# Block inverses of a delta rule by one VectorE transpose instead of through DRAM, with longer allowances for small transfers

## The chip, the core and the metric

The kernel runs on one core of a Trainium2 chip. The core has a TensorE (PE; its weight loads are shown apart as PEld), a VectorE (DVE), a ScalarE (ACT), a GpSimd (POOL) and a SyncE (SP), which here only issues DMAs. The engines run on their own and wait for each other through semaphores. The metric is the device time of one execution in microseconds (us); lower is better.

## The reference

One decoder layer on 512 positions of width 1024, in float32: `h = x + 1/2 FFN1(norm(x))`, `h = h + mixer(norm(h))`, `h = h + 1/2 FFN2(norm(h))`, and a last norm. Each FFN is a SwiGLU with an inner width of 2816. The mixer projects `h` to many columns, runs two recurrences over the positions, projects each one's output back, merges the two with sigmoid gates and projects once more. One recurrence is HGRN2 with 8 heads. The other, the gated delta rule, has 16 value heads over 8 query/key heads of width 128 and is cut to:

```python
# q, k, v in chunks of C = 64 positions; gam = cumsum(g), L = exp(gam_t - gam_s) for s <= t
A = strict_lower((k * beta) @ k.T * L)
T = inverse(eye + A)                       # unit lower triangular, one per head and chunk
u = T @ (v * beta)
w = T @ (k * beta * exp(gam))
qk = q @ k.T * L
for each chunk:                            # S: 128 x 128, carried along
    v_new = u - w @ S
    o = (q * exp(gam)) @ S + qk @ v_new
    S = S * exp(g_end) + k_to_end.T @ v_new
```

The change is about `T`. The mathematics are the same before and after.

## The kernel before, in words

Every large product is made of three float32r products: each operand is split into a high and a low part (`uh`, `ul`; `whi`, `wlo`), and `mm3` (lines 164 to 166) issues high x high, low x high and high x low, a "triple". Weights come from HBM in slabs of 128x512 (`raw`); ScalarE casts the high part (L1394 in the mixer, L159 outside of it) and VectorE subtracts it for the low part (L1396, L160). Three `raw` buffers and five pairs of split slabs are in flight.

The mixer is one long list of work, made on the host while the program is built. Each activity is a Python generator that yields what it needs next: `"get"` a buffer, `"on"` an event, `"use"` an engine for an estimated time, or `"lag"`, a time that passes without an engine, which stands for a DMA in flight. The class `Desk` plays these generators against a clock of its own and issues each instruction when its engine is free by that clock. So the estimates decide only the order in which each engine's instructions stand. On the chip each engine runs its own list strictly in that order and waits where something is not there yet. `LAG` holds the times for transfers. `SLACK = 0.8` lets TensorE's steps other than the large products stand 0.8 us later than the clock says they are ready. The thread `product` fills TensorE with projections wherever no other step is ready; `loader` and `maker` bring its slabs.

The delta rule works on eight units `u` of two value heads, in four blocks of 128 positions. Of a unit these activities touch the change:

- `g_e` loads the decay sums broadcast to all partitions (`gb`, L796) and makes `exp(-|gb - gam|)` of them on ScalarE (L801, L804).
- `g_n` makes the negated strict lower matrix `n2` on VectorE (L874).
- `g_b` inverts the 32x32 diagonal blocks. Four DMAs store the diagonal blocks to DRAM (`nb`, L893), four load them back spread over partitions (`m`, shown as `gfs`, L899), and one loads a piece of the identity (`t`, shown as `ft`, L904). GpSimd then runs 31 steps of substitution of two instructions each (L910, L911). After it a DMA of GpSimd stores `t` to DRAM (`nt`, L914), and four of SP load it with rows and columns exchanged (`tq`, shown as `gln`, L923).
- `g_inv` waits for that. VectorE copies it into `tp` (L947) and transposes each of four 32-row groups into `ut` (L954); ScalarE copies pieces (L960). Two levels of small products on TensorE (L971, L981, L994, L1002), with copies between them on ScalarE (L974, L984, L996, L1005), join the inverted blocks, first two of 32 rows and then two of 64.
- `g_rec` is the recurrence over the four blocks, with `pw`, `pog`, `pks` for its accumulators (L1056 to L1085), VectorE's scaling (L1074), and at its end the output norm and two transposes `pto` on TensorE (L1129) that go to DRAM by `keep` (L1151).

Other activities with small transfers are `tgate` (L1162, L1165: gates `tg`, stored by `keep`), `branch` (`yh`, stored by `keep`), `operand` (loads a stored head output `og`, L1200, and splits it, L1206 and L1208) and `merged` (loads `mi`, `mt`, `mg`, L1227 to L1233, and merges, L1236 to L1242). `claim` hands buffers of the HGRN2 heads to the delta rule once those are done.

Of the kernel before, what the change touches and what calls it, by code (L numbers as in the profile page):

```python
# [8 lines left out]
F32 = mybir.dt.float32  # L9
# [7 lines left out]
P = 128  # L17
T = 512
NT = T // P
D = 1024  # L20
# [20 lines left out]
WB = 5  # L41
TA = 6
RB = 3
KEEP = 2
CONVS = 5
SLACK = 0.8
LAG = dict(raw=3.2, gb=4, nb=5, m=6, nt=4, tq=8, out=4)
EASE = 2.5
LANES = {"a": 2, "b": 2, "d": 1, "e": 1}

# [319 lines left out]
def mixer(tc, mp, e):  # L370
# [67 lines left out]
    od = dr.tile([VH, P, T], F32, name="od")  # L438


    D = Desk(mm=2, a=2, b=2, d=1, e=1, ta=TA, tm=6, thg=1, raw=RB, w=WB, tq=1, n2=2, gz=2, fs=1, ut=1, kn=3, gm=1,
             qm=2, gb=2, ln=1, mi=3, mt=3, at=4, vb=4, t64=2, on=2, ft=1, x=1, we=1, w_=1, s=3)
    V = lambda n: ("use", "DVE", 0.21 + 0.001 * n)
    A = lambda n: ("use", "ACT", 0.2 + 0.0009 * n)
# [439 lines left out]
    def g_b(u, st):  # L884


        n2 = st["n2"]
        nb = dr.tile([4, 8, 32, 32], F32, name=f"nb{u}")
        nt = dr.tile([4, 32, 32, 8], F32, name=f"nt{u}")
        for b in range(4):  # L890
            r = slice(32 * b, 32 * b + 32)
            yield S
            sp.dma_start(nb[b].rearrange("s i j -> i s j"), n2[r, :, :, r].rearrange("p a c j -> p (a c) j"))  # L893
        yield "lag", LAG["nb"]
        yield "on", *([("P", u - 1)] if u else ["m"])
        m = G["m"][0]
        for b in range(4):
            yield S
            sp.dma_start(m[32 * b:32 * b + 32].rearrange("p i j -> p (i j)"),  # L899
                         nb[b].rearrange("s i j -> s (i j)").unsqueeze(0).to_broadcast([4, 8, 1024]))  # L900
        yield "get", "ft", 1
        t = places["ft"]("ft", (P, 32, 8))
        yield S
        sp.dma_start(t, eye4)  # L904
        yield "lag", LAG["m"]
        for j in range(31):
            n, w = 31 - j, j // 4 + 1
            yield "use", "POOL", .7 + .004 * n * w
            tv = v3(places["fm"]("fm", (P, 96))[:, :n * w], n)
            pool.tensor_tensor(tv, bc(m[:, j + 1:, j], w), t[:, j:j + 1, :w].to_broadcast([P, n, w]), op=ALU.mult)  # L910
            pool.tensor_tensor(t[:, j + 1:, :w], t[:, j + 1:, :w], tv, op=ALU.add)  # L911
        D.fire(("P", u))
        yield "use", "POOL", .6
        pool.dma_start(nt.rearrange("b q i c -> (b q) i c"), t)  # L914
        yield "lag", LAG["nt"]
        D.put("ft")
        D.fire(("T", u))
        yield "on", "tq"
        yield "get", "tq", 1
        tq = st["tq"] = G["tq"][0]  # L920
        for b in range(4):
            yield S
            sp.dma_start(tq[32 * b:32 * b + 32], nt[b].rearrange("q i c -> i q c"))  # L923
        yield "lag", LAG["tq"]
        D.fire(("B", u))

    def g_w(u, i, st):
        yield "on", ("v", 2 * u + i), ("C", u)
# [10 lines left out]

    def g_inv(u, st):  # L940

        yield "on", ("B", u), *([("I", u - 1)] if u else []), *([("K", u - 3)] if u > 2 else []), \
            ("ut", u % 3), ("t64", u % 2), *(["more"] if u else [])
        n2 = st["n2"].rearrange("p a c b -> p (a c) b")
        tp = G["tp"][u % 2]
        yield V(256)
        dve.tensor_copy(tp.rearrange("p s (c g) -> p s c g", g=4), st["tq"].rearrange("p (g s) c -> p s c g", g=4))  # L947
# [243 lines left out]
    def operand(k, wait, get, make):  # L1191

        yield "on", *wait
        if get:
            yield "get", get, 2
        yield "on", ("od", k), *([("so", k - 2)] if k > 10 else [])
        yield "get", "ta", 1
        yield S
        og = ta("og")
        sp.dma_start(og, od[k])  # L1200
        yield "lag", LAG["raw"]
        if k > 8:
            yield "on", "projected"
        yield *A(512), 1
        a, b = so[k] = make()
        act.copy(a, og)  # L1206
# [14 lines left out]
    def merged(d):  # L1221
# [64 lines left out]
    def claim(name, tag, n, shape, zero=False):  # L1286

        G.setdefault(name, [])
        yield "on", ("free", tag)
        for j in range(n):  # L1290
            yield "get", "w_" if tag == "w" else tag, 1
            G[name].append(pl(tag, shape))
            if zero:
                yield "use", "POOL", 1.0
                pool.memset(G[name][-1], 0.0)
            if tag == "ln":
                D.fire("tq")
            elif tag == "fs":
                D.fire("m")
            else:  # L1300
                D.fire((name, j))
# [197 lines left out]
        D.start((2, i), h_pair(i))  # L1499
    for name, tag, n, shape in (("kn", "kn", 3, tb), ("qm", "qm", 2, tb), ("n2", "n2", 2, big),  # L1500
                                ("gz", "gz", 2, (P, NT, 256)), ("at", "at", 4, tb), ("vb", "vb", 4, tb),
                                ("m", "fs", 1, (P, 32, 32)), ("tq", "ln", 1, (P, 32, 8)), ("x", "x", 1, col),
                                ("we", "we", 1, col), ("w", "w", 1, col)):
        D.start((6, 0), claim(name, tag, n, shape))
    D.start((6, 0), claim("ut", "ut", 1, (P, 8, P), True))
# [106 lines left out]
```

## Time and profile before

| | |
|---|---|
| median of 3 runs | 1676.11 us (1674.88 to 1676.27) |
| profiled execution | 1671.58 us |
| its span, first to last instruction | 1669.8 us |
| mean granted TensorE clock | 0.994 |
| busy share of the span | PE 98%, PEld 83%, DVE 58%, ACT 42%, POOL 19% |
| DMA | 181.21 MB in 141223 packets, 53008 of them under 512 B |

The mixer's slabs are loaded from 357.1 us on (L1377); its last output, by the product with `wo` (L1536), is added to `h` at 1292.3 us. In the profile a line "engine line out<-in" names an instruction by its output and input tiles; `SPq` and `POOLq` are the queues in which DMAs are issued. An entry in brackets, `[4.56 <-DVE gut L954]`, gives the idle time of the engine just before the instruction and what ended it. A row of waits has the total, the number and the longest. Busy shares are averages over stages with different limits, and on an engine which is not the limit idle time costs nothing.

### The profile page before, as it was taken

Reading aid. Unit: us, or ns where it says so; the run is one execution under the profiler, and the core shown is the slowest. Engines: PE = TensorE matmul, PEld = TensorE weight load, DVE = VectorE, ACT = ScalarE, POOL = GpSimd, SP = SyncE. Lnnn points to the kernel's source line nnn. Section 1 sums busy time; section 2 is a strip of 40 time slices with the busy share of each in tenths; the row PEclk is TensorE's granted clock in tenths of the full one; section 3 lists DMA queues with packets and bytes.
Section 4 is the critical chain, followed back from the end, with each engine's and each line's share of the span. In section 5 each row is a group of like instructions: output and inputs, shape, how many; then the busy total and the mean of one; then the engine's idle time right before and its main releaser. Section 6 shows DMA issues by size and latency. Waiting matters only on the chain. (4 is left out here: it accounts for less than half of the span.)

```text
span 1669.8 us, 27534 instructions
## 1 busy us (share of the span) xinstructions
PE 1640.4 (98%) x10130; PEld 1392.4 (83%) x10130; DVE 969.9 (58%) x2000; ACT 699.3 (42%) x1547; POOL 322.1 (19%) x637
## 2 busy tenths in 40 slices
PE   8999999999999999989999999999999999999997
PEld 6888888888888898868988888887888888888886
DVE  5544443337677777648878888755445444444333
ACT  5333332333334346446665565554224333333332
POOL 2000000001121221461655346600001000000001
PEclk9999999999999999999999999999999999999998
DMA  5232233332212222543344343445544232223333
GB/s 175 90 100 95 96 97 108 117 119 71 77 65 63 79 83 77 154 132 80 112 111 117 112 121 109 137 141 183 160 150 133 90 100 95 98 98 92 98 98 108
DMA packets 141223, 181.21 MB, mean 109 GB/s; under 512 B 53008, under 2 KB 58640, under 8 KB 141088
## 3 DMA queue, kind: packets, MB, share of 16 engines
q1 hardware_dynamic: 140272, 177.78, 34.4%
q8 instruction: 80, 1.31, 0.3%
q0 software_dynamic: 384, 1.05, 0.2%
q10 hardware_dynamic: 432, 0.62, 0.1%
q14 instruction: 55, 0.45, 0.1%
HBM read 163.11 MB, written 16.29 MB: 107 GB/s over the span
## 5 line engine op out<-in xcount | busy, mean ns | idle before, releaser
L164 PE MATMUL pmm<-uh,whi 128*128 128x512 f32 (+1 forms) x1280 | 516.4, 404 | 10.2 <-ACT whi L301 6.9
L166 PE MATMUL pmm<-uh,wlo 128*128 128x512 f32 (+1 forms) x1280 | 501.5, 392 | 0.0
L165 PE MATMUL pmm<-ul,whi 128*128 128x512 f32 (+1 forms) x1280 | 501.2, 392 | 0.0
L159 ACT CAST whi<-raw 128x512 fp32r<-128x512 f32 (+1 forms) x290 | 176.5, 609 | 404.9 <-PE pmm L165 382.9
L160 DVE TENSOR_TENSOR wlo<-raw,whi 128x512 fp32r<-128x512 f32 (+1 forms) x290 | 203.1, 702 | 243.3 <-ACT whi L159 242.6
L164 PEld LDWEIGHTS pmm<-uh,whi 128*128 128x128 f32 (+1 forms) x1280 | 241.4, 189 | 59.7 <-ACT whi L301 7.4
L166 PEld LDWEIGHTS pmm<-uh,wlo 128*128 128x128 f32 (+1 forms) x1280 | 241.0, 188 | 52.5 <-DVE wlo L302 0.5
L165 PEld LDWEIGHTS pmm<-ul,whi 128*128 128x128 f32 (+1 forms) x1280 | 241.6, 189 | 46.4
L1396 DVE TENSOR_TENSOR wlo<-raw,whi 128x512 fp32r<-128x512 f32 x241 | 168.5, 700 | 150.4 <-ACT whi L1394 143.2
L1394 ACT CAST whi<-raw 128x512 fp32r<-128x512 f32 x241 | 149.3, 620 | 244.5 <-PE pmm L165 160.1
L202 POOL TENSOR_TENSOR acc<-acc,sqt 128x512 f32<-128x512 f32 x24 | 32.4, 1352 | 805.6 <-ACT sqt L200 805.3
L164 PE MATMUL pnat<-whi,uh 128*128 128x256 f32 x512 | 155.2, 303 | 0.0
L166 PE MATMUL pnat<-whi,ul 128*128 128x256 f32 x512 | 144.7, 283 | 0.0
L165 PE MATMUL pnat<-wlo,uh 128*128 128x256 f32 x512 | 144.5, 282 | 0.0
L164 PE MATMUL pmm<-gh,whi 128*128 128x512 f32 (+1 forms) x374 | 141.0, 377 | 0.0
L166 PE MATMUL pmm<-gh,wlo 128*128 128x512 f32 (+1 forms) x374 | 140.9, 377 | 0.0
L165 PE MATMUL pmm<-gl,whi 128*128 128x512 f32 (+1 forms) x374 | 140.8, 377 | 0.0
L910 POOL TENSOR_TENSOR fm<-gfs,ft 128x60 f32<-128x60 f32 (+24 forms) x248 | 95.9, 387 | 127.7 <-DMA ft<-hmask 89.0
L911 POOL TENSOR_TENSOR ft<-ft,fm 128x60 f32<-128x60 f32 (+24 forms) x248 | 99.3, 400 | 19.4
L164 PEld LDWEIGHTS pnat<-whi,uh 128*128 128x128 f32 x512 | 97.6, 191 | 2.1
L165 PEld LDWEIGHTS pnat<-wlo,uh 128*128 128x128 f32 x512 | 97.8, 191 | 0.8
L166 PEld LDWEIGHTS pnat<-whi,ul 128*128 128x128 f32 x512 | 97.5, 190 | 0.0
(384 smaller groups left out, 2180.4 us busy)
## 6 DMA issues: line engine op xcount, KB each, us to landing
raw<-wt SPq DMA_DIRECT2D x128, 256.0 KB
raw<-w1b SPq DMA_DIRECT2D x88, 256.0 KB
raw<-w1a SPq DMA_DIRECT2D x86, 256.0 KB
raw<-wn SPq DMA_DIRECT2D x64, 256.0 KB
raw<-w2b SPq DMA_DIRECT2D x45, 256.0 KB
raw<-w2a SPq DMA_DIRECT2D x40, 256.0 KB
raw<-wbg SPq DMA_DIRECT2D x32, 256.0 KB
gb<-gtd SPq DMA_DIRECT2D x16, 256.0 KB
```

The source lines that it names most:

```text
L159: act.copy(hi[:, :f], raw[:, :f])
L160: dve.tensor_tensor(lo[:, :f], raw[:, :f], hi[:, :f].bitcast(F32), op=ALU.subtract)
L164: pe.matmul(pt, ah, bh, start=first, stop=False)
L165: pe.matmul(pt, ah, bl, start=False, stop=False)
L166: pe.matmul(pt, al, bh, start=False, stop=last)
L202: pool.tensor_tensor(acc, acc, s, op=ALU.add)
L910: pool.tensor_tensor(tv, bc(m[:, j + 1:, j], w), t[:, j:j + 1, :w].to_broadcast([P, n, w]), op=ALU.mult)
L911: pool.tensor_tensor(t[:, j + 1:, :w], t[:, j + 1:, :w], tv, op=ALU.add)
L1394: act.copy(hi, raw)
L1396: dve.tensor_tensor(lo, raw, hi.bitcast(F32), op=ALU.subtract)
```

## The change

After GpSimd's last step, `t` holds in each group of 32 partitions four column groups `g` by eight matrices `s`, and on the free axis 32 rows by eight columns. Now one VectorE transpose, which works in blocks of 32x32, reads `t` with its free axes exchanged and writes the rows to partitions and `(c, g, s)` straight into `tp`. The store `nt`, the loads `tq` and the copy are gone. `t` has three buffers now (`t0` in the place of `ft`, two in `t12` in the place where `tq` was) and is given back after the transpose. `g_inv` waits for the event `P`, which is fired behind GpSimd's last step, instead of `B`.

The allowances change too: `raw` from 3.2 to 3.5, `gb` from 4 to 6.5, `nb` from 5 to 6, `m` from 6 to 7, `out` from 4 to 5; `nt` and `tq` go; and the loads of `operand` and `merged`, which were given `raw`, are given a time of their own, `back`, of 6.

```diff
-LAG = dict(raw=3.2, gb=4, nb=5, m=6, nt=4, tq=8, out=4)
+LAG = dict(raw=3.5, gb=6.5, nb=6, m=7, out=5, back=6)
...
-    D = Desk(mm=2, a=2, b=2, d=1, e=1, ta=TA, tm=6, thg=1, raw=RB, w=WB, tq=1, n2=2, gz=2, fs=1, ut=1, kn=3, gm=1,
+    D = Desk(mm=2, a=2, b=2, d=1, e=1, ta=TA, tm=6, thg=1, raw=RB, w=WB, n2=2, gz=2, fs=1, ut=1, t=3, kn=3, gm=1,
...
         nb = dr.tile([4, 8, 32, 32], F32, name=f"nb{u}")
-        nt = dr.tile([4, 32, 32, 8], F32, name=f"nt{u}")
...
-        yield "get", "ft", 1
-        t = places["ft"]("ft", (P, 32, 8))
+        yield "on", ("t12", 0) if u % 3 else ("t0", 0)
+        yield "get", "t", 1
+        t = st["t"] = G["t12"][0][:, u % 3 - 1] if u % 3 else G["t0"][0]
         yield S
         sp.dma_start(t, eye4)
         yield "lag", LAG["m"]
...
         D.fire(("P", u))
-        yield "use", "POOL", .6
-        pool.dma_start(nt.rearrange("b q i c -> (b q) i c"), t)
-        yield "lag", LAG["nt"]
-        D.put("ft")
-        D.fire(("T", u))
-        yield "on", "tq"
-        yield "get", "tq", 1
-        tq = st["tq"] = G["tq"][0]
-        for b in range(4):
-            yield S
-            sp.dma_start(tq[32 * b:32 * b + 32], nt[b].rearrange("q i c -> i q c"))
-        yield "lag", LAG["tq"]
-        D.fire(("B", u))
...
-        yield "on", ("B", u), *([("I", u - 1)] if u else []), *([("K", u - 3)] if u > 2 else []), \
+        yield "on", ("P", u), *([("I", u - 1)] if u else []), *([("K", u - 3)] if u > 2 else []), \
...
         yield V(256)
-        dve.tensor_copy(tp.rearrange("p s (c g) -> p s c g", g=4), st["tq"].rearrange("p (g s) c -> p s c g", g=4))
-        D.put("tq")
+        dve.transpose(tp.rearrange("p s (c g) -> p c g s", g=4), st["t"].rearrange("p i c -> p c i"))
+        D.put("t")
...
         sp.dma_start(og, od[k])
-        yield "lag", LAG["raw"]
+        yield "lag", LAG["back"]
...
         sp.dma_start(g, td[8 + d])
-        yield "lag", LAG["raw"]
+        yield "lag", LAG["back"]
```

In the list of buffers that `claim` hands over, `("tq", "ln", 1, (P, 32, 8))` becomes `("t0", "ft", 1, (P, 32, 8))` and `("t12", "ln", 1, (P, 2, 32, 8))`.

More of the change, by code (lines that the diff above doesn't have):

```diff
@@ L1295, in claim @@
                 pool.memset(G[name][-1], 0.0)
-            if tag == "ln":
-                D.fire("tq")
-            elif tag == "fs":
+            if tag == "fs":
                 D.fire("m")
@@ L1501, in mixer @@
                                 ("gz", "gz", 2, (P, NT, 256)), ("at", "at", 4, tb), ("vb", "vb", 4, tb),
-                                ("m", "fs", 1, (P, 32, 32)), ("tq", "ln", 1, (P, 32, 8)), ("x", "x", 1, col),
+                                ("m", "fs", 1, (P, 32, 32)), ("t0", "ft", 1, (P, 32, 8)), ("t12", "ln", 1, (P, 2, 32, 8)), ("x", "x", 1, col),
                                 ("we", "we", 1, col), ("w", "w", 1, col)):
```

## The prediction

> **What bounds the kernel now.** I read the page first, then the waits of TensorE, then the stretches in which it waited, then the four engines in time around the longest wait.
>
> ```profile
> span 1669.8 us, 27534 instructions
> PE 1640.4 (98%) x10130; PEld 1392.4 (83%) x10130; DVE 969.9 (58%) x2000; ACT 699.3 (42%) x1547; POOL 322.1 (19%) x637
> ```
>
> The page says TensorE is busy in 98% of the span. Busy is no proof of work without gaps, so the waits come next (engine and line, what it waited for, us in total, times, longest).
>
> ```profile
> PE pmm L164 <- ACT whi L301: 6.9, 1, 6.9
> PE pq L971 <- DVE gut L954: 5.2, 2, 4.6
> PE pmm L164 <- DVE tg L1162: 2.4, 1, 2.4
> PE pog L1083 <- DVE x L1074: 1.7, 1, 1.7
> PE pq L981 <- ACT acc L974: 1.5, 1, 1.5
> ```
>
> The wait on L301 lies in the first stage, which the diff doesn't touch. The other four lie in the mixer, and they are all that TensorE waits for there, so the change can gain only these four, what the clock adds to them, and whatever it does to the order of the products. Here are the four stretches (stretch; PE busy, PEld, DVE, ACT, POOL; granted clock, DMA share, GB/s).
>
> ```profile
> 700.00:750.00 50.00, 44.77 (x259) 35.94 (x258) 23.66 (x41) 21.59 (x49) 35.10 (x88) 0.93 0.44 130
> 850.00:900.00 50.00, 48.50 (x404) 44.35 (x404) 40.95 (x96) 32.07 (x95) 29.09 (x70) 1.00 0.34 92
> 1000.00:1050.00 50.00, 48.29 (x393) 43.36 (x392) 42.77 (x98) 26.59 (x78) 28.96 (x70) 1.00 0.38 107
> 1150.00:1200.00 50.00, 47.64 (x207) 38.99 (x206) 28.19 (x48) 18.04 (x31) 0.00 (x0) 0.97 0.53 168
> ```
>
> TensorE lacks 5.2, 1.5, 1.7 and 2.4 us of the 50, and in the first and the last stretch the clock fell too, to 0.93 and 0.97 on average. Why the longest one came about is seen engine by engine: SP's queue, then ScalarE, then VectorE, then TensorE (start, us, instruction, idle before it and releaser).
>
> ```profile
> 721.18 5.87 SPq L923 DMA_DIRECT2D gln<-nt  x4
> 728.18 0.42 SPq L796 DMA_DIRECT2D gb<-gtd  x1
> ```
> ```profile
> 733.09 1.28 ACT L801 ACTIVATE x<-gb,gx 128x128 f32<-128x128 f32 x4 [5.59 <-DMA gb<-gtd]
> ```
> ```profile
> 735.57 0.69 DVE L1396 TENSOR_TENSOR wlo<-raw,whi 128x512 fp32r<-128x512 f32 x1 [5.61 <-ACT whi L1394]
> 736.29 1.36 DVE L954 STREAM_TRANSPOSE gut<-gtp 32x256 f32<-32x256 f32 x3
> ```
> ```profile
> 736.78 0.24 PE L971 MATMUL pq<-gut,gn 32*32 32x32 f32 x2 [4.56 <-DVE gut L954]
> 737.70 1.05 PE L971 MATMUL pq<-gut,gn 32*32 32x32 f32 x30 [0.68 <-DVE gut L954]
> 739.28 0.63 PE L165 MATMUL pmm<-ul,whi 128*128 128x512 f32 x1
> 739.71 0.63 PE L166 MATMUL pmm<-uh,wlo 128*128 128x512 f32 x1
> 743.55 0.63 PE L166 MATMUL pmm<-uh,wlo 128*128 128x512 f32 x1
> 745.06 0.39 PE L165 MATMUL pmm<-ul,whi 128*128 128x512 f32 x1
> 745.29 0.40 PE L166 MATMUL pmm<-uh,wlo 128*128 128x512 f32 x1
> ```
>
> Four small loads `gln<-nt`, which bring the first block inverse back from DRAM, hold SP's queue for 5.87 us. The load `gb<-gtd` behind them is issued at 728.18. ScalarE comes to its consumer L801 and stands 5.59 us. The slabs' casts are behind it, VectorE stands 5.61 us for a cast, three of the four transposes of the same block inverse are behind that, and TensorE, at the first product of the inverse, stands 4.56 and then 0.68 us. After that the products are slow: from 739.28 to 743.55 lie ten intervals between starts, 0.43 us each, and from 745.06 to 745.29 it is 0.23 us.
>
> The other three waits have the same root, a small transfer that landed after its consumer's turn in the list:
>
> ```profile
> ACT gat L801 <- DMA gb<-gtd: 5.5, 2, 3.3
> 1036.67 0.62 ACT L1206 CAST sogm<-og 128x512 fp32r<-128x512 f32 x1 [2.71 <-DMA og<-od]
> 1039.32 0.35 DVE L1074 TENSOR_SCALAR x<-pw,gx 128x128 f32<-128x128 f32 x1 [0.44 <-ACT x L1026]
> DVE tg L1162 <- DMA td<-tg: 5.6, 1, 5.6
> ```
>
> ScalarE waited twice more for `gb`, up to 3.3 us, and L974, for which the products at L981 waited 1.5 us, is in its queue behind one of these. The 2.7 us for `og` end at 1036.67, L1074 follows on VectorE at 1039.32, and TensorE's 1.7 us at L1083 are put down to L1074; that `og` is their root I infer from the times. The 5.6 us that VectorE stood for the store `td<-tg` precede the 2.4 us at L164 directly: the step that reads the accumulator out was waiting for room. The list allows 4 us for `gb`, 3.2 for `og` and 4 for the store.
>
> **The change, part by part.** Its first part takes the way through DRAM out.
>
> ```profile
> L947 DVE COPY gtp<-gln x4: 381/386/395, 729.1 to 1045.8; 128x256 f32<-128x256 f32 x4
> L947 DVE COPY x<-gln x4: 371/384/391, 773.6 to 1090.0; 128x256 f32<-128x256 f32 x4
> L954 DVE STREAM_TRANSPOSE gut<-gtp x8: 432/435/442, 729.5 to 1047.6; 32x256 f32<-32x256 f32 x8
> L914 POOL DMA_DIRECT2D nt<-ft x8: 625/626/759, 716.0 to 1079.5; - x8
> L923 SPq DMA_DIRECT2D gln<-nt x32: 319/562/3493, 721.2 to 1084.4; - x32
> ```
>
> Removed are 8 stores (L914), 0.626 us of GpSimd each, 5.0 us in all; 32 loads on SP (L923), 0.56 us each in the median and up to 3.49; and 8 copies of 0.385 us on VectorE. Added are 8 transposes of 128x256. Their nearest row is the transpose of 32x256 at 0.435 us with as many elements per partition, so VectorE gains 8 x 0.05 = 0.4 us of work; it is 47% to 86% busy in the stretches above, and the estimate's ends are 0.385 us (the copy's price) and four times 0.435 us (if the four groups of 32 partitions went one after the other), which would be +10.8 us on VectorE, 1.35 us a unit, mostly in slack. I take 0.435 as the instruction handles all partitions like the copy does.
>
> The latency it removes is longer: from the issue of the store to the copy were 13.1 us in the first unit (716.0 to 729.1) and 10.5 in the last (1079.5 to 1090.0). That is no gain by itself, as TensorE had other products to do. But the four loads block no `gb` any more, and this wait goes too:
>
> ```profile
> SPq L923 <- DMA nt<-ft: 10.6, 3, 4.2
> ```
>
> SP stood 10.6 us for the stores, with slab loads behind it; those had cover in five slab buffers, so I cost this at nothing.
>
> The second part is the new times. `gb` gets 6.5 us instead of 4, `og` and the merge's three loads 6 instead of 3.2, stores 5 instead of 4, slabs 3.5 instead of 3.2, and the loads before GpSimd's loop 6 + 7 instead of 5 + 6. None of these makes an engine wait by itself; they move the consumers later in the list and let other products go ahead. TensorE's order still has 7,533 rows against 7,535, so the work is the same; 8 DMA issues leave GpSimd's order.
>
> What each wait is worth: the first is 4.56 + 0.68 us, and the ten slow intervals, 4.27 us instead of 2.3, so 2.0, with some 0.7 (an estimate) for the products at both edges of the slow stretch: 7.9. The second 1.5, the third 1.7. The fourth is 2.4 and the clock: 0.97 over 50 us is 3 us at half speed, so 1.5 us of work lost: 3.9. Sum 15.0 us. For the fourth the new allowance looks short: VectorE's wait for the store alone is 5.6 us, and stores are given 5. [...]
>
> What is new: the first transpose of a unit now waits for GpSimd's last step directly, where 10.5 to 13.1 us lay between. It is issued in VectorE's strict order, with the slabs' subtractions behind it, for which TensorE waits.
>
> ```profile
> L910 POOL TENSOR_TENSOR fm<-gfs,ft x248: 203/303/838, 686.9 to 1078.7; 128x60 f32<-128x60 f32 x12, 128x54 f32<-128x54 f32 x8, 128x66 f32<-128x66 f32 x8, 128x28 f32<-128x28 f32 x8
> L911 POOL TENSOR_TENSOR ft<-ft,fm x248: 204/318/870, 687.2 to 1079.0; 128x60 f32<-128x60 f32 x12, 128x54 f32<-128x54 f32 x8, 128x66 f32<-128x66 f32 x8, 128x28 f32<-128x28 f32 x8
> ```
> ```profile
> 893.27 0.25 POOL L910 TENSOR_TENSOR fm<-gfs,ft 128x31 f32<-128x31 f32 x1 [15.54 <-DMA ft<-hmask]
> 896.92 1.66 POOL L1112 TENSOR_TENSOR sm<-sm,mhalf 128x8 f32<-128x8 f32 x1
> 911.39 1.47 POOL L840 TENSOR_TENSOR sm<-sm,mhalf 128x4 f32<-128x4 f32 x1
> 927.24 0.21 POOL L911 TENSOR_TENSOR ft<-ft,fm 128x8 f32<-128x8 f32 x1
> ```
>
> A loop of 31 pairs is given 31 x 0.7 + 0.004 x 1560 = 27.9 us in the list (L909). The first took 29.1 us (686.9 to the store at 716.0): 1.2 us over. The one from 893.27 to 927.45 took 34.2, with the two powers shown and a small product of other units inside, which the list gives 3.4 us: 2.9 over. Against it, 2 us more are given ahead of each loop for its loads. So I take VectorE to wait 1 us at half of the units. Before TensorE sees it, four transposes (1.7 us) and copies stand in between, and the list leaves 0.8 us ahead of such products. Taken as 0.3 us of TensorE for each of 8 units, 2.4 us; its ends are 0 and 8 x 2.9 = 23 us. The last unit has less behind it: in the new order 17 of the triples of products of the last projection stand ahead of its second output transpose, against 6 before, and 10 instead of 21 between that transpose and the product which needs it. At 3 x 0.23 us a triple that is 7 us of cover left instead of 14, more than the overrun of 2.9 us, so I cost it at nothing.
>
> **Sum.** 15.0 removed, 2.4 added: 12.6 us less. The profiled execution took 1671.58 us (1669.8 of span), so 1659.0 by it. The three runs shown have a median of 1676.11, 4.5 us more, which no row explains; I put the same difference on the median: 1663.5.
>
> **Rivals.**
> VectorE waits for GpSimd: the strict order that made 4.56 us of TensorE's wait out of a late `gb` now has a late loop at the same place, eight times. It decides from 15.0 / 8 = 1.9 us of TensorE a unit on. At the 2.9 us overrun with nothing hidden, 23.2 us are added, and 1676.1 - 15.0 + 23.2 = 1684. For it speaks that L911 takes 0.87 us at most and 0.32 in the median, so loops stretch; against it, that the loops start earlier relative to the list by up to 2 us, and that 1.7 us of VectorE's own transposes lie between its wait and TensorE's first product of the unit. [...]
>
> Other transfers come late: every list draws new neighbours, and a few of the many small transfers were late enough before. If three such waits of 2.4 + 1.5 us come anew (the price of the fourth), 11.7 us are added: 1675 (1663.5 + 11.7). For it speaks the 5.6 us store against 5; against it, that `gb` is given 6.5 us where the one above took 4.9 from issue to use (728.18 to 733.09), and that SP's 5.87 us block is gone.
>
> The change doesn't do what it says: if the waits come from the load of SP and DMA and not from the allowance, only the first goes, 7.9 us: 1668. That is inside my range.
>
> **How the numbers follow.** Waits go, with few new ones: 0.76, from 15.0 us less to 7.5 less (half of it), 1661 to 1669. Late transfers: 0.10, 1673 to 1679. VectorE behind GpSimd: 0.14, 1680 to 1690. What a measurement of this kernel can tell from no change is about 0.2%, 3.4 us: 1672.8 to 1679.5. Faster is the first case and a little of the second, 0.78; same 0.08; slower 0.14. The range runs from 1658, under the full gain by the spread of the runs, to 1678; it leaves out the third case and the ends of the others.
>
> **What would show it.** In the profile after, TensorE's waits for `gut`, `acc` and `tg` are gone or under 1 us, the clock in 700:750 and 1150:1200 is 1.00, the new transposes take about 0.44 us and VectorE's idle time before them, put down to GpSimd, is under 10 us in all. Wrong would be: a TensorE wait of over 2 us behind a unit's transposes, a dip of the clock between 680 and 1170 us, or a unit's loop that ends over 3 us behind the place of its transpose.

## The result, and the profile after

Six executions of the changed kernel have a median of 1662.64 us (1660.81 to 1665.11), against 1675.39 us (1672.22 to 1676.27) for six of the kernel before. The ratio is 0.9928, with a 95% interval from 0.9915 to 0.9941: 12.75 us less by the medians. The profiled execution took 1662.14 us, 9.4 us less than that of before (1671.58).

The page's head and its busy times:

```profile
span 1660.4 us, 27417 instructions
PE 1636.5 (99%) x10130; PEld 1388.8 (84%) x10130; DVE 973.2 (59%) x2000; ACT 699.3 (42%) x1547; POOL 323.8 (19%) x629
```

TensorE's busy time is 3.9 us shorter (1640.4 before) with as many products, which fits fewer of them at half clock: in the mixer the granted clock was 0.50 for 6.83 and 3.41 us before, and is so for 3.41 us now. The waits of TensorE, the three that lie in the mixer:

```profile
PE pmm L164 <- DVE tg L1149: 1.9, 1, 1.9
PE pgq L859 <- DVE gvb L923: 1.9, 1, 1.9
PE pks L1043 <- DVE s L1083: 1.7, 1, 1.7
```

The waits for `gut` (5.2 us), for `acc` (1.5) and at the old L1083 (1.7) are gone. The one for `tg` is still there (2.4 before), and two are new. The same stretches as before (PE, PEld, DVE, ACT, POOL; clock, DMA share, GB/s):

```profile
700.00:750.00 50.00, 50.00 (x317) 41.04 (x316) 27.20 (x59) 23.60 (x61) 31.77 (x85) 1.00 0.42 129
850.00:900.00 50.00, 48.34 (x405) 44.20 (x405) 37.08 (x95) 27.59 (x81) 22.21 (x56) 1.00 0.29 86
1000.00:1050.00 50.00, 50.00 (x447) 43.25 (x446) 43.72 (x99) 30.31 (x88) 28.80 (x62) 1.00 0.34 96
1150.00:1200.00 50.00, 48.07 (x210) 39.29 (x209) 27.53 (x47) 15.55 (x27) 0.00 (x0) 0.97 0.55 169
```

The first stretch went from 44.77 us at a clock of 0.93 to a full 50.00 at 1.00, the third from 48.29 to 50.00. The second lacks 1.66 us in place of 1.5, but from another cause, and the fourth is nearly what it was.

The new transposes on VectorE (ns, least/median/longest), and VectorE's idle time ahead of them (us, times):

```profile
L934 DVE STREAM_TRANSPOSE x<-gln x3: 680/696/701, 747.9 to 1088.2; 128x256 f32<-128x256 f32 x3
L934 DVE STREAM_TRANSPOSE gtp<-gft x2: 693/704/716, 708.1 to 1034.2; 128x256 f32<-128x256 f32 x2
  POOL gft L911: 3.8, 2
  POOL gln L911: 2.7, 2
```

A transpose takes 0.70 us. At four of the eight units VectorE stood for GpSimd, 6.5 us in all. What that does to TensorE is seen at the two units where it costs most (start, us, instruction, idle before it and releaser):

```profile
869.80 0.20 POOL L911 TENSOR_TENSOR gft<-gft,fm 128x8 f32<-128x8 f32 x1
870.04 0.70 DVE L934 STREAM_TRANSPOSE x<-gft 128x256 f32<-128x256 f32 x1 [2.23 <-POOL gft L911]
872.76 0.70 PE L1043 MATMUL pks<-s,h 128*128 128x256 f32 x2 [1.66 <-DVE s L1083]
...
927.39 0.70 DVE L934 STREAM_TRANSPOSE gtp<-gln 128x256 f32<-128x256 f32 x1 [2.56 <-POOL gln L911]
931.33 0.69 DVE L923 TENSOR_TENSOR gvb<-ptv,sm 128x512 f32<-128x512 f32 x1
932.16 1.10 PE L859 MATMUL pgq<-h 128*128 128x256 f32 x4 [1.87 <-DVE gvb L923]
```

VectorE stands 2.23 and 2.56 us until GpSimd's last step is done, and starts 0.04 us behind it. What TensorE then waits for isn't the block inverse. It is other work in VectorE's list behind the transpose: a scaling of the recurrence's state (L1083), and `gvb` of another activity (L923). 1.66 and 1.87 us of the 2.23 and 2.56 arrive at TensorE.

The fourth wait, SP's queue first:

```profile
1139.66 0.42 SPq L1214 DMA_DIRECT2D mi<-md  x1
...
1144.48 0.55 SPq L1220 DMA_DIRECT2D mg<-td  x1
1145.12 0.61 SPq L1369 DMA_DIRECT2D raw<-wbg  x1
1146.11 0.40 SPq L1138 DMA_DIRECT2D td<-tg  x1
```
```profile
1152.48 0.69 DVE L1149 TENSOR_TENSOR tg<-pmm,rbc 128x512 f32<-128x512 f32 x1 [2.51 <-DMA td<-tg]
1153.32 0.47 PE L164 MATMUL pmm<-sogb,whi 128*128 128x512 f32 x1 [1.93 <-DVE tg L1149]
1156.49 0.63 PE L166 MATMUL pmm<-sogm,wlo 128*128 128x512 f32 x1
```

From 1139.66 to 1144.48 SP issues nine loads of `merged` (the first and the last are shown). The store `td<-tg` is issued behind them at 1146.11, and what waits for it goes on at 1152.48, 6.4 us later. Then products are slow again, 0.63 us each where they take 0.39 at full clock: the granted clock is 0.50 from 1153.77 to 1157.16 us.

### The profile page after: what moved, and what is told of

It reads as the page before. It is cut to its first block, busy times and chain, and to the rows that moved or that the text cites. A ratio compares the mean times of both kernels' runs of the same rounds, so it can differ in the third digit from the quotient of the medians.

```text
span 1660.4 us, 27417 instructions
## 1 busy us (share of the span) xinstructions
PE 1636.5 (99%) x10130; PEld 1388.8 (84%) x10130; DVE 973.2 (59%) x2000; ACT 699.3 (42%) x1547; POOL 323.8 (19%) x629
## 5 line engine op out<-in xcount | busy, mean ns | idle before, releaser
L164 PEld LDWEIGHTS pmm<-gh,whi 128*128 128x128 f32 x374 | 70.4, 188 | 13.0
L165 PEld LDWEIGHTS pmm<-gl,whi 128*128 128x128 f32 x374 | 70.4, 188 | 12.8
```

What stands on the lines that cost most here:

```text
L164: pe.matmul(pt, ah, bh, start=first, stop=False)
L165: pe.matmul(pt, ah, bl, start=False, stop=False)
```

## The experiments

Each kernel was compared with the kernel before on its own chip, and the ratio stands with its 95% interval. Where two changed kernels are compared, it is by these ratios, as shares of 1675 us. Two theories were open. By the first, the gain comes from the way of the data: without the loads through DRAM, SP's queue isn't blocked and the waits end. By the second, it comes from the list: the longer allowances put late consumers further back, and the transpose itself is neutral or a loss, as it takes away GpSimd's cover.

### The allowances alone, and the transpose alone

The kernel before, with its way through DRAM and all the new allowances:

```diff
-LAG = dict(raw=3.2, gb=4, nb=5, m=6, nt=4, tq=8, out=4)
+LAG = dict(raw=3.5, gb=6.5, nb=6, m=7, nt=4, tq=8, out=5, back=6)
...
         sp.dma_start(og, od[k])
-        yield "lag", LAG["raw"]
+        yield "lag", LAG["back"]
...
         sp.dma_start(g, td[8 + d])
-        yield "lag", LAG["raw"]
+        yield "lag", LAG["back"]
```

> The kernel before with the new allowances alone; the block inverses still go through DRAM. If the allowances do most of the work (each late transfer got more time), TensorE's waits for gut, acc and tg shrink to under 4 us in all and the time falls by 8 to 12 us against before. If the DRAM path is the root (the four loads gln<-nt hold SP's queue for up to 5.9 us in front of a gb load), the first wait stays, with its dip of the clock, and the time falls by 3 to 7 us.

The changed kernel with the old allowances:

```diff
-LAG = dict(raw=3.5, gb=6.5, nb=6, m=7, out=5, back=6)
+LAG = dict(raw=3.2, gb=4, nb=5, m=6, out=4, back=3.2)
```

> The changed kernel with the old allowances (raw 3.2, gb 4, nb 5, m 6, out 4, and 3.2 for the loads back). If the DRAM path is the root, the long wait at the first unit goes and 5 to 8 us are gained against before. If the allowances matter, waits of 1.5 to 5 us behind gb, og and the stores stay; and as GpSimd's loop has 2 us less in front of it in the list, VectorE waits for GpSimd about 2 us at most units, so that the time is within 4 us of before or over it.

| | old allowances | new allowances |
|---|---|---|
| through DRAM | 1 (before) | 0.9954 [0.9940, 0.9969] |
| one transpose | 1.0063 [1.0048, 1.0078] | 0.9928 [0.9915, 0.9941] (after) |

The allowances alone take 7.3 us off (1673.43 to 1666.16), a little less than the 8 to 12 expected. The transpose alone adds 11.4 us (to 1684.87). Together they take 12 us off, so the parts don't add up: under the old allowances the transpose costs 11 us, under the new ones it gains some 4 (there the two intervals just touch, so this is at the edge of what the runs can tell).

TensorE's largest wait in the mixer with the allowances alone, and ScalarE's for `gb`; the next lines are VectorE's, and then TensorE's, with the transpose alone:

```profile
PE pq L981 <- ACT acc L974: 3.3, 2, 1.9
ACT gat L801 <- DMA gb<-gtd: 5.0, 1, 5.0
```
```profile
DVE x L934 <- POOL gln L911: 4.6, 3, 2.8
DVE gtp L934 <- POOL gft L911: 3.6, 1, 3.6
DVE gtp L934 <- POOL gln L911: 3.4, 1, 3.4
DVE x L934 <- POOL gft L911: 2.7, 1, 2.7
```
```profile
PE pq L968 <- ACT acc L961: 4.8, 1, 4.8
PE pks L1043 <- DVE s L1083: 4.8, 3, 2.1
PE pmm L164 <- DVE tg L1149: 3.1, 1, 3.1
```

With the allowances alone the wait of 4.56 us in the first unit is gone although the four loads through DRAM are still there (issued at 714.27 us, they hold SP's queue for 5.57 us). But in this order no load of `gb` stands close behind them: the next one is issued at 745.7 us. So the longer allowances, all of them together, end that wait by moving its parts away from each other. Which of them does it isn't shown, nor that the block would be harmless with a `gb` behind it. Later a `gb` still comes late: ScalarE stands 5.0 us for it until 847.77, and one of the two waits at L981 (1.4 us) is behind that.

With the transpose alone VectorE stands 14.3 us for GpSimd, at all eight units it starts right behind the loop, and late `gb` (8.0 us on ScalarE) and `og` (5.5 us) are back. TensorE's waits of over 0.4 us in this mixer are 19.0 us in all. Only 5.4 us of them (0.4, 0.9, 2.1 and 2.0 us) follow a transpose that stood for GpSimd. The longest, 4.8 us, is behind `og`, and the others are behind `gb`, late slabs and the store of `tg`. So most of what the transpose loses under the old allowances is lost to late transfers.

### A later loop, and less lead ahead of it

How much of GpSimd's lateness arrives at TensorE? In the first kernel of the two, GpSimd gets eight multiplications more in each unit's loop. They write into scratch, the list isn't told, and the order on every other engine stays as it was.

```diff
             pool.tensor_tensor(t[:, j + 1:, :w], t[:, j + 1:, :w], tv, op=ALU.add)
+            for _ in range(8 if j == 15 else 0):
+                pool.tensor_tensor(v3(places["fm"]("fm", (P, 96))[:, :64], 16), bc(m[:, 16:, 15], 4),
+                                   t[:, 15:16, :4].to_broadcast([P, 16, 4]), op=ALU.mult)
```

> The changed kernel with eight idle multiplications in each of GpSimd's eight loops, about 3 us a unit, which the list is not told of: the order on all other engines is the same. If each us that GpSimd is late reaches TensorE (the rival of the prediction, 8 x 2.9 us with nothing hidden), the time rises by 20 us or more against the changed kernel, to 1683 or above. If most of it is hidden by VectorE's transposes and the list's reserves, as the sum had it (0.3 us a unit at 1 us of lateness), it rises by 5 to 12 us, with TensorE waits of 1 to 2 us at most units.

```profile
L913 POOL TENSOR_TENSOR fm<-gfs,gln x40: 292/292/841, 737.5 to 1108.9; 128x64 f32<-128x64 f32 x40
```

The median is 1686.36 us, 1.0070 [1.0052, 1.0087], some 24 us over the changed kernel. The loops took 30.5 to 37.3 us, where the changed kernel's take 27.2 to 33.8: 3.5 us longer on the mean, 28 us over the eight units. TensorE in the mixer (680 to 1100 us), first in the changed kernel, then here:

```profile
680.00:1100.00 420.00, 416.43 (x2972) 359.54 (x2971) 321.19 (x737) 240.29 (x669) 219.40 (x516) 1.00 0.38 115
```
```profile
680.00:1100.00 420.00, 398.88 (x2778) 343.18 (x2777) 302.34 (x697) 225.47 (x626) 222.07 (x529) 0.98 0.33 104
```

3.6 us of idle time become 21.1, and the clock falls too (this profiled execution, at 1692.77 us, is the slowest of its four). By the medians some 24 of the 28 us arrive in the time, partly as idle time of TensorE and partly as slower clock. VectorE stands 25.5 us at the transposes, and 10.7 us more at L845 for a small power (L840) that GpSimd has in the same list as its loops; in the changed kernel it doesn't stand there.

The second kernel takes away only the 2 us by which the changed kernel starts each loop's loads earlier against its consumers:

```diff
-LAG = dict(raw=3.5, gb=6.5, nb=6, m=7, out=5, back=6)
+LAG = dict(raw=3.5, gb=6.5, nb=5, m=6, out=5, back=6)
```

> The changed kernel, with only the two allowances ahead of GpSimd's loop put back (nb 5, m 6 instead of 6 and 7); all others are the new ones. If these 2 us are what keeps the direct wait for GpSimd short, VectorE's waits for GpSimd rise from 6.4 us in all to 12 to 16 us (14.3 with all the old allowances) and the time rises by 6 to 14 us against the changed kernel. If the loss of the transpose with the old allowances came from gb, og and the stores, it stays within 3 us.

1672.29 us, 0.9979 [0.9970, 0.9988]: 8.5 us of the gain are lost. VectorE's wait for GpSimd is 7.8 us instead of 6.5, which doesn't account for that. The longest new wait comes another way. SP's wait in total, its queue, then ScalarE and TensorE:

```profile
SPq L898 <- POOL gln L911: 8.3, 2, 4.8
```
```profile
827.64 2.61 SPq L898 DMA_DIRECT2D gfs<-nb  x4
830.34 0.40 SPq L1362 DMA_DIRECT2D raw<-wt  x1
837.50 0.62 ACT L1379 CAST whi<-raw 128x512 fp32r<-128x512 f32 x1 [4.89 <-DMA raw<-wt]
841.11 1.06 PE L968 MATMUL pq<-acc,gtp 32*32 32x32 f32 x32 [4.01 <-ACT acc L961]
```

The next unit's loads of `m` go into the buffer that the running loop still reads, so SP stands until GpSimd's last step has read it (827.6). The slab load behind them is issued 2.7 us later still, ScalarE stands 4.89 us for a slab, its copy `acc` is behind that cast, and TensorE stands 4.01 us. That this slab is the one issued at 830.34 is inferred from the times. So a late loop has two ways to TensorE: VectorE's list, and SP's queue. SP's total at this place is 6.0 us in the changed kernel, 8.3 here, and 16.1 in the kernel with the longer loops. Of the two edits that take a part of the new allowances back (this one, and that of `gb` below), this one cost more. It also gives TensorE another order, so how much of the 8.5 us is the lead's own isn't shown.

### The time for the other transfers

`gb` back to 4 us, in the first kernel; stores up to 8 us, in the second:

```diff
-LAG = dict(raw=3.5, gb=6.5, nb=6, m=7, out=5, back=6)
+LAG = dict(raw=3.5, gb=4, nb=6, m=7, out=5, back=6)
```

> The changed kernel with 4 us for gb instead of 6.5, all else new. If the gb allowance is what took the two longest waits away (the first of 4.56 and 0.68 us with its slow clock, and the one of 1.5 us stood behind gb in the kernel before), ScalarE waits for gb again by 3 to 8 us in all and the time rises by 4 to 9 us against the changed kernel. If it was SP's block by the loads from DRAM, which is gone here too, it stays within 2 us.

```diff
-LAG = dict(raw=3.5, gb=6.5, nb=6, m=7, out=5, back=6)
+LAG = dict(raw=3.5, gb=6.5, nb=6, m=7, out=8, back=6)
```

> The changed kernel with 8 us instead of 5 for stores. The wait for a store td<-tg behind nine loads of the merge (1.93 us of TensorE and a dip of the clock that costs 1.5 us in the changed kernel; it stands in every profile taken so far but that with the new allowances and the DRAM path) should go, and the time falls by 2 to 4 us against the changed kernel. If a list drawn anew brings other waits of the same size, it stays within 2 us.

With `gb` at 4 us the median is 1663.53 us, 0.9938 [0.9921, 0.9955]. ScalarE waits for `gb` again (4.1 and 2.4 us), and no TensorE wait in the mixer is over 1.8 us. That is 1 to 2 us against the changed kernel, not a clear difference. So this allowance is worth little once the way through DRAM is gone, although a `gb` still comes late: in the first unit 6.4 us lie between its issue (722.2) and its use (728.6), with no block ahead of it. What the allowance is worth beside the way through DRAM wasn't run alone. VectorE stands 11.7 us for GpSimd here, against 6.5, and hardly any time is lost: in another order such lateness needn't arrive.

With 8 us for stores the median is 1662.68 us, 0.9918 [0.9903, 0.9933], like the changed kernel, and the fourth wait is still there (2.1 us). TensorE, VectorE and ScalarE have the same order as in the changed kernel: this allowance moves nothing there, and it isn't what makes the fourth wait.

The loads of `merged` ahead of the store make it. In this kernel the loads of `merged` are held back until the last projection is done:

```diff
-        yield "on", ("K", 7), ("y", d), ("t", d), ("t", 8 + d), *([("ms", d - 3)] if d > 2 else [])
+        yield "on", "projected", ("K", 7), ("y", d), ("t", d), ("t", 8 + d), *([("ms", d - 3)] if d > 2 else [])
```

> The changed kernel, with the merge's loads (mi, mt, mg) held back in the list until the projections are done. In the changed kernel nine of these loads stand in SP's queue in front of a store td<-tg, and three of them hold buffers that the gates tg share; VectorE then waits 2.51 us for that store and TensorE 1.93 us, and the clock dips for 3.4 us. If these loads are the cause, the wait and the dip go and the time falls by 2 to 4 us against the changed kernel. A longer allowance for stores left the wait where it was; if something else holds the buffer, it stays here too.

```profile
1150.00:1200.00 50.00, 48.61 (x215) 39.09 (x214) 29.48 (x51) 17.03 (x29) 0.00 (x0) 1.00 0.61 205
```

The wait for `tg` is gone and the clock is 1.00, but 1.3 us of small waits for `og` come in its place (L1193, L1195), and the median is 1662.50 us, 0.9927 [0.9912, 0.9942]. So the loads of `merged` cause the fourth wait. They put traffic ahead of the store, and three of them hold buffers out of the six that the gates use too; this edit takes both away, so which of the two makes the wait stays open. That its end brings time by itself isn't shown either.

### The price of the transpose

Ahead of each transpose stand two more here, written into the same place and overwritten by the real one: one that reads and writes in order (L935), and one that only reads with exchanged axes (L936). The real one is L937.

```diff
+        flat = tp.rearrange("p s x -> p (s x)")
+        dve.transpose(flat, st["t"].rearrange("p i c -> p (i c)"))
+        dve.transpose(flat.rearrange("p (c i) -> p c i", c=8), st["t"].rearrange("p i c -> p c i"))
         dve.transpose(tp.rearrange("p s (c g) -> p c g s", g=4), st["t"].rearrange("p i c -> p c i"))
```

> The changed kernel with two more transposes of t in front of the real one, on VectorE, which overwrites what they write: one reads and writes 128x256 elements in order, one reads with exchanged axes and writes in order. The list is not told, so the order of the other engines is the same. If the 0.70 us of the new transpose (0.435 was predicted, from 32 partitions) come from its strided reads and writes, the first takes about 0.44 and the second lies between; if they come from 128 partitions, all three take 0.70. The price: 1.1 to 1.4 us of VectorE a unit, 9 to 11 us in all; hidden, the time rises by under 2 us; if VectorE's lateness passes to TensorE as GpSimd's 3 us did, by 5 to 11 us.

```profile
L935 DVE STREAM_TRANSPOSE x<-gln x3: 436/445/447, 748.9 to 1099.9; 128x256 f32<-128x256 f32 x3
L936 DVE STREAM_TRANSPOSE x<-gln x3: 667/680/685, 749.3 to 1100.4; 128x256 f32<-128x256 f32 x3
L937 DVE STREAM_TRANSPOSE x<-gln x3: 684/693/734, 750.0 to 1101.1; 128x256 f32<-128x256 f32 x3
```

128 partitions cost hardly more than 32: 0.445 us against 0.435. The exchanged read adds 0.24 us, the strided write next to nothing on top of it. The median is 1668.48 us, 0.9957 [0.9943, 0.9972]: 9.0 us more on VectorE (8 x 1.12) cost some 5 us. GpSimd's loops are 3.4 us longer in all here, so a part of the 5 us may come through them.

So `t` was kept column by column, for the transpose to read in order. GpSimd then steps over 128 bytes from element to element:

```diff
-    eye4 = e["hmask"][:, 5:9].rearrange("p a (i c) -> p (a i) c", c=8)
+    eye4 = e["hmask"][:, 5:9].rearrange("p a (c i) -> p (a c) i", i=32)
...
         sp.dma_start(t, eye4)
+        t = t.rearrange("p c i -> p i c")
...
-        dve.transpose(tp.rearrange("p s (c g) -> p c g s", g=4), st["t"].rearrange("p i c -> p c i"))
+        dve.transpose(tp.rearrange("p s (c g) -> p c g s", g=4), st["t"])
...
-    eye4 = np.eye(32).reshape(32, 8, 4).transpose(2, 0, 1)
+    eye4 = np.eye(32).reshape(32, 8, 4).transpose(2, 1, 0)
```

> The changed kernel with t kept column by column, so that the new transpose reads in order; GpSimd's steps read and write it with a stride of 128 bytes instead. The transpose should take 0.44 us instead of 0.70 (the probe: 0.445 in order, 0.68 with exchanged reads). If VectorE's delay at that place passes on, 8 x 0.26 us are to be had at most, 0 to 2 us; if GpSimd's steps get slower by the stride, its loops of 27 to 34 us grow, and as 3.3 us a loop cost 24 us, each 0.3 us of a loop costs about 2 us.

GpSimd's addition, in the changed kernel and then here:

```profile
L911 POOL TENSOR_TENSOR gln<-gln,fm x155: 203/317/841, 717.9 to 1088.0; 128x60 f32<-128x60 f32 x15, 128x28 f32<-128x28 f32 x10, 128x54 f32<-128x54 f32 x10, 128x48 f32<-128x48 f32 x10
```
```profile
L912 POOL TENSOR_TENSOR gln<-gln,fm x155: 209/357/933, 719.8 to 1106.5; 128x60 f32<-128x60 f32 x15, 128x28 f32<-128x28 f32 x10, 128x54 f32<-128x54 f32 x10, 128x48 f32<-128x48 f32 x10
L935 DVE STREAM_TRANSPOSE x<-gln x3: 622/646/659, 751.3 to 1106.8; 128x256 f32<-128x256 f32 x3
```

The transpose falls only to 0.65 us, as its writes are strided alone now. GpSimd's addition rises from 0.317 to 0.357 us in the median, its multiplication from 0.297 to 0.356, the loops are 1.1 to 3.7 us longer (29.2 to 36.3), 16.5 us over the eight units, and the median is 1676.48 us, 1.0014 [1.0001, 1.0027]: 14 us more. Again most of GpSimd's lateness is paid, under the same order of TensorE.

### An allowance where the new wait is, and a control

Between GpSimd's last step and the transpose the list has no time at all now. This kernel gives it 2.5 us:

```diff
         D.fire(("P", u))
+        yield "lag", 2.5
+        D.fire(("B", u))
...
-        yield "on", ("P", u), *([("I", u - 1)] if u else []), *([("K", u - 3)] if u > 2 else []), \
+        yield "on", ("B", u), *([("I", u - 1)] if u else []), *([("K", u - 3)] if u > 2 else []), \
```

> The changed kernel with 2.5 us more in the list between GpSimd's last step and the transpose. In the changed kernel VectorE waited 2.23 and 2.56 us for GpSimd ahead of two transposes, and TensorE 1.66 and 1.87 us behind them. If these came from GpSimd being late, both go and the time falls by 3 to 4 us against the changed kernel (about 1659). If a new list merely draws other waits, it stays within 2 us of it, with waits at other places.

```profile
PE pmm L164 <- DVE tg L1151: 3.0, 1, 3.0
PE pq L970 <- ACT acc L963: 2.7, 1, 2.7
SPq L898 <- POOL gln L911: 3.5, 1, 3.5
840.95 0.62 ACT L1381 CAST whi<-raw 128x512 fp32r<-128x512 f32 x1 [4.07 <-DMA raw<-wt]
```

Both new waits are gone, and VectorE's idle time for GpSimd falls from 6.5 to 0.6 us. But the list came out otherwise. The wait of 2.7 us ends at 842.01 and has the form found above: SP stands 3.5 us until a loop has read `m` (828.6), ScalarE stands 4.07 us for a slab, and the copy `acc` is behind that cast; that the slab is late by SP's wait is inferred from the times. An allowance ahead of the transpose doesn't touch this way. The fourth wait is 3.0 us, and the median is 1664.87 us, 0.9945 [0.9930, 0.9960], no better.

As a control, the slabs' allowance was moved by 0.1 us, which changes 20 places in TensorE's order:

```diff
-LAG = dict(raw=3.5, gb=6.5, nb=6, m=7, out=5, back=6)
+LAG = dict(raw=3.6, gb=6.5, nb=6, m=7, out=5, back=6)
```

> A control: the changed kernel with 3.6 instead of 3.5 us for slabs, which no transfer needs. It only draws another order. If the gain belongs to the allowances and the transpose, the time stays within 4 us of the changed kernel. If it was the luck of one order, it differs by more, up to the 12 us of the gain.

1663.05 us, 0.9928 [0.9911, 0.9944], with the same three waits (1.7, 2.2 and 2.1 us). The gain doesn't hang on one lucky order, at least not near this one.

### A version that beats both

It takes a smaller allowance ahead of the transpose, a larger one for `gb`, and the late merge:

```diff
-LAG = dict(raw=3.5, gb=6.5, nb=6, m=7, out=5, back=6)
+LAG = dict(raw=3.5, gb=8, nb=6, m=7, out=5, back=6)
...
         D.fire(("P", u))
+        yield "lag", 1.5
+        D.fire(("B", u))
...
-        yield "on", ("P", u), *([("I", u - 1)] if u else []), *([("K", u - 3)] if u > 2 else []), \
+        yield "on", ("B", u), *([("I", u - 1)] if u else []), *([("K", u - 3)] if u > 2 else []), \
...
-        yield "on", ("K", 7), ("y", d), ("t", d), ("t", 8 + d), *([("ms", d - 3)] if d > 2 else [])
+        yield "on", "projected", ("K", 7), ("y", d), ("t", d), ("t", 8 + d), *([("ms", d - 3)] if d > 2 else [])
```

> Three edits on the changed kernel together: 1.5 us more in the list between GpSimd's last step and the transpose, 8 us for gb, and the merge's loads held back. If the three remaining waits are each curable (3.5 us behind GpSimd, 1.9 and 1.5 us behind the store), it takes 5 to 7 us less than the changed kernel, about 1656. If each new list brings new waits, it stays within 3 us of it.

```profile
680.00:1100.00 420.00, 420.00 (x3018) 363.42 (x3017) 325.28 (x746) 243.65 (x676) 214.78 (x517) 1.00 0.37 116
```

TensorE has no gap between 680 and 1100 us, and what is left of waits in the mixer is 0.8 us in all. No transpose waits for GpSimd. The median is 1656.89 us (1656.04 to 1657.12), 0.9892 [0.9877, 0.9907]: 18 us under before and 6 under the changed kernel. Which of the three edits does what isn't separated: the late merge alone and 2.5 us ahead of the transpose alone brought nothing, and 8 us for `gb` alone wasn't run.

## Why the prediction was right, and where it was not

The forecast was 1663.5 us, and 1662.64 was measured. The sum behind it is right in its largest part, the first three waits. That the number came out within 1 us is partly luck: by the rows of the two profiles the waits give 8.1 us instead of 12.6, the two profiled executions differ by 9.4, and the rest of the 12.75 us between the medians stands in no row.

| step | forecast, us | what the profile shows |
|---|---|---|
| first wait, with its clock | -7.9 | gone; 700 to 750 us is full, clock 1.00 |
| second and third wait | -1.5 and -1.7 | gone |
| fourth wait, with its clock | -3.9 | 1.9 us of 2.4 are left, and the clock of 0.97: -0.5 |
| VectorE behind GpSimd | +2.4 | 1.66 + 1.87 = +3.5 |
| sum | -12.6 | -8.1 |

**Waits go, and what caused them.** The first three went as forecast. The reason given for the first, the blocked queue, is only one part of it. The loads through DRAM did hold SP's queue, but with these loads still there the allowances end that wait too, by an order in which no `gb` stands behind the block. The rival by which only the first wait would go falls with this: second and third went as well. Taking out the way through DRAM, costed at nothing beyond its blocked queue, is worth some 4 us under the new allowances, if the two touching intervals are taken at their middle.

**The fourth wait.** "-3.9" is a step that failed. The text had said that 5 us looked short for a store that kept VectorE 5.6 us, and yet counted the wait as removed. A longer allowance doesn't move it either; the loads of `merged` ahead of the store do.

**VectorE behind GpSimd.** Forecast were 1 us at half of the units, and 0.3 us of TensorE at each of eight; measured are 6.5 us of VectorE at four units and 3.5 us of TensorE at two. The sum of this term was near, but its reasoning was wrong: it took the four transposes and copies and the list's 0.8 us for a cover that hides most of the lateness. TensorE waits not for the inverse but for VectorE's work behind the transpose, or for slabs that SP loads late, and neither has such a cover. Under the same order, 28 us more lateness made the time 24 us longer, and 16.5 us made it 14 longer. What kept the term small are the allowances that came along, the lead of 2 us ahead of each loop among them: without it 8.5 us are gone, though VectorE's wait for GpSimd hardly grows (7.8 us). So the rival of the other sign was nearer than a chance of 0.14 says. The transpose alone is 11.4 us slower, but there late transfers, the second rival, make more of TensorE's waits than GpSimd does. The spread of L911, on which the rival leaned, isn't one of shapes alone: of the 24 instructions of 128x60 in the kernel before, 17 took 0.30 to 0.31 us and seven 0.63 to 0.87. What makes these seven slow, no run here shows.

**The new transpose** was taken at 0.435 us and takes 0.70. That is 2.1 us more on VectorE over eight units (8 x 0.265), inside the ends that were given. By the kernel with two more transposes, where 9.0 us cost some 5, it is worth about 1 us of time (an estimate).

**Late transfers.** The rival with three new waits of this kind didn't come about; in the changed kernel ScalarE waits at most 1.0 us for `gb`. With the transpose and the old allowances it did.

**The last unit's cover**, costed at nothing: no wait of the last unit is among TensorE's.

**The median.** 4.5 us lay between the profiled execution of before and its median, put down to no row. The granted clock is a likely place: it was 0.994 in that execution, and in 13 others of the same kernel on one chip it went from 0.996 in the fastest (1668.64 us) to 0.992 and 0.993 in the slowest (up to 1676.62). The six executions of the changed kernel have 0.995 to 0.997. Each 0.001 of the span's mean clock is 1.7 us, which is what one stretch of 3.4 us at half speed costs. That would also be why the medians differ by 12.75 us where the rows give 8.1: the waits of before cost more clock in most executions than in the profiled one. No run isolates this.

Of the signs named in advance, the clock of 1.00 in the first stretch, `gut` and `acc` without a wait and under 10 us of VectorE's idle time came true. `tg` under 1 us, a transpose of 0.44 us and no dip of the clock before 1170 us did not. The two other signs of being wrong didn't come: TensorE's waits behind a transpose stay under 2 us, and no loop ended over 3 us late.

## What to carry to other kernels

Where a list is ordered by estimates, a slow way is also a cover: taking it out makes a late producer couple directly to the consumer's engine, and what stalls is whatever stands behind in that engine's list (here 2.23 and 2.56 us of VectorE made 1.66 and 1.87 of TensorE). So the edit that shortens a path has to bring an allowance at the place of the new wait (alone it brought nothing here, together with two other edits 6 us), and a small lead ahead of the producer can be worth more than the shortened path (here 8.5 us, with the order it brings, against some 4). Look for the new wait by following the idle engine's list, not the data. An engine's busy share doesn't tell what its time is worth: GpSimd was busy 19% of the span, and making its steps longer cost 14 us, while the longer transpose on VectorE is worth about 1 (the estimate above).

## What the runs showed of the hardware

**The clock doesn't go by the length of the gap alone.** Mean clock around two gaps of TensorE, in the kernel with 8 us for stores (gaps of 2.17 us at 932.78 and 2.10 at 1153.80) and then in the control (2.19 at 932.58, 2.07 at 1154.36):

```profile
930.00:940.00 10.00, 7.83 (x92) 5.86 (x91) 7.96 (x24) 4.15 (x11) 1.85 (x2) 1.00 0.32 103
1150.00:1160.00 10.00, 7.91 (x28) 6.07 (x27) 5.50 (x14) 2.22 (x4) 0.00 (x0) 0.83 0.69 230
```
```profile
930.00:940.00 10.00, 7.82 (x91) 5.82 (x90) 7.79 (x23) 3.94 (x11) 1.85 (x2) 1.00 0.30 104
1150.00:1160.00 10.00, 7.93 (x36) 6.28 (x35) 6.98 (x16) 2.95 (x7) 0.00 (x0) 1.00 0.75 254
```

The gap of 2.10 us cost clock (0.83 over 10 us), those of 2.17, 2.19 and 2.07 us did not. What sets them apart, these views don't show.

The profiles of before and, in the second block, of after show when the clock changed, to 0.02 us:

```profile
736.00:737.25 1.25, 0.24 (x2) 0.13 (x2) 1.17 (x4) 1.23 (x5) 1.06 (x3) 1.00 0.00 0
737.27:744.08 6.81, 6.38 (x42) 4.72 (x42) 6.13 (x11) 4.80 (x12) 5.93 (x11) 0.50 0.39 116
744.10:746.00 1.90, 1.90 (x39) 1.64 (x39) 0.27 (x1) 0.51 (x1) 1.54 (x5) 1.00 0.37 139
1152.00:1153.68 1.68, 0.26 (x1) 0.29 (x2) 1.10 (x2) 0.32 (x1) 0.00 (x0) 1.00 0.20 77
1153.70:1157.09 3.39, 3.39 (x9) 2.67 (x8) 3.27 (x8) 1.56 (x4) 0.00 (x0) 0.50 0.37 115
1157.11:1159.00 1.89, 1.89 (x10) 1.52 (x9) 1.58 (x5) 0.99 (x2) 0.00 (x0) 1.00 0.43 121
1657.00:1658.85 1.85, 0.00 (x0) 0.00 (x0) 1.37 (x4) 0.42 (x1) 1.14 (x2) 1.00 0.61 202
1658.87:1669.80 10.93, 2.67 (x10) 2.28 (x10) 2.21 (x6) 0.37 (x1) 2.78 (x4) 0.50 0.46 158
```
```profile
1152.00:1153.75 1.75, 0.43 (x2) 0.42 (x3) 1.27 (x3) 0.49 (x1) 0.00 (x0) 1.00 0.38 135
1153.77:1157.16 3.39, 3.39 (x10) 2.64 (x9) 2.61 (x8) 0.62 (x2) 0.00 (x0) 0.50 0.71 204
1157.18:1159.00 1.82, 1.82 (x9) 1.47 (x9) 0.65 (x2) 0.62 (x1) 0.00 (x0) 1.00 0.58 196
1650.00:1652.09 2.09, 0.83 (x6) 0.74 (x6) 0.28 (x2) 0.42 (x1) 0.29 (x1) 1.00 1.01 344
1652.11:1660.30 8.19, 1.22 (x4) 0.93 (x4) 2.05 (x5) 0.37 (x1) 2.48 (x4) 0.50 0.42 146
```

In the mixer the half clock lasted 6.827 us (from 737.26) and 3.413 us (from 1153.69) before, and 3.413 us (from 1153.76) after. These stretches stand behind TensorE's gaps of 4.56 and 0.68, of 2.36 and of 1.93 us. Behind the gaps of 1.50 and 1.71 us (before) and of 1.66 and 1.87 us (after) the clock stayed at 1.00.

The three stretches of before start 416.43 and 505.17 us apart, which is 122 and 148 times 3.413 us. In steps of 3.413 us laid from these starts, and likewise from those of after (498.35 us apart, 146 times), TensorE was idle for 3.17, 2.36 and 2.48 us of the step ahead of a start before, and for 1.93 and 2.58 us after. No other step from 20 us on, in either profile, has more than 1.71 us. So in these two profiles the idle time within a step separates the cases; the 1.87 us, for one, are cut by a border into 1.59 and 0.28. No run isolates this, and for the four gaps of 2.07 to 2.19 us it isn't shown.

Nor does it take one long gap. With the allowances alone TensorE's idle time from 1150 to 1200 us is 2.7 us, in waits of 0.9 us at most, and the clock fell to 0.93:

```profile
1150.00:1200.00 50.00, 47.27 (x198) 37.60 (x197) 26.88 (x53) 16.29 (x36) 2.26 (x2) 0.93 0.57 192
```

**A strided read made VectorE's transpose half as long again** (0.445 to 0.68 us for 128x256 in float32), a strided write alone nearly as much (0.65), and both together hardly more than one (0.69). GpSimd pays 0.04 us for an addition and 0.06 us for a multiplication, in the median, for a step of 128 bytes.
